# Expert blocks of over 64 rows: three fp32r passes over split operands, and a shorter ring of weights

## The chip, the cores and the metric

One Trainium2 chip, one core. The time is device microseconds of one execution of the whole program. An unchanged kernel's executions shown here lie between 2280.43 and 2285.77 us.

## What is computed

Two networks of two layers each run one after the other on 256 tokens of width 1024. The first network's layers have attention and then a mixture of experts; the second's have a mixer and a plain feed-forward. The change touches the experts alone. What they compute, from the reference:

```
def hier_moe(h, w_group, b_group, w_router, b_router, w1, w3, w2):
    ...                      # pick one of 4 groups, then 2 of its 8 experts, for each row of h
    def expert_block(a):
        xb, e = a            # up to 128 rows that chose expert e
        return (jax.nn.silu(xb @ w1[e]) * (xb @ w3[e])) @ w2[e]
    ...
    return jnp.zeros((t, d), h.dtype).at[tok_s].add(w_s[:, None].astype(h.dtype) * yb[dest])
```

There are 32 experts; w1 and w3 are 1024x512, w2 is 512x1024, all fp32. Layer 0 routes 512 rows (tokens and context), layer 1 routes 256, two experts to a row. How many rows an expert gets is known only during the run.

## The kernel before

**Stages.** build (L1623) runs layer 0's attention, its expert stage (moe_scope, L1580), layer 1's attention, its expert stage, and the second network. Inside moe_scope, route_tokens (L764) counts the rows of each expert and orders the experts: the even places from 2 on hold the large ones in falling size, the odd places small ones. Then experts (L984) goes through them with branches on the counts, all written out in a row: turn (L1117) takes an expert through tc.If; `small` (up to 64 rows: half1/half2 or, up to 32, quarter1/quarter2) or `large` (full1/full2 for 128 rows, and `rest` for each further 128).

**A full block.** full1 multiplies 128 gathered rows (xT, transposed, 8 slices of 128) with w1 (m = 0) and w3 (m = 1): 16 products of 128x128 by 128x512 into two PSUM banks (L1073). ScalarE takes Silu of the first bank (L1076), VectorE multiplies by the second (L1077). `between` runs next_rows, which transposes the next expert's rows (L997) and copies them to SBUF on ScalarE (L999). Four transposes (L1081) and a copy (L1082) make hT, and full2 multiplies it with w2 in 8 products (L1088); ScalarE and VectorE copy the result out (L1091, L1092) and GpSimd scatters it (L1002). All operands are plain fp32.

**Weights.** An expert's weights are six pieces of 128x2048 fp32, 1 MB each, loaded by SyncE's queue (wpiece, L139). The buffers are a ring (wtile, L132): WRING = 6 of a pool that lives for the whole program and nx more of one that lives for the expert stage, so 16 in layer 0 and 18 in layer 1. A piece is loaded when the buffer's last reader is through; for a large expert, whose readers stand in branches, that is the end of those branches.

**Order.** Instructions of one engine run in the order in which the program holds them. The tile framework fixes that order at build time by a simulated timeline: of what is ready it issues what was written first. Instructions inside a branch don't mix with those outside.

**The same arithmetic elsewhere.** The dense stages already use three passes: dense (L154) copies a weight to fp32r on ScalarE (L166), VectorE subtracts that from the weight to get the low part (L167), and mm3 (L176) adds high x high, high x low and low x high (L178 to L180):

```
    def mm3(self, out, xh, xl, wh, wl, start, stop):
        mm = self.nc.tensor.matmul
        mm(out, lhsT=xh, rhs=wh, start=start, stop=False)
        mm(out, lhsT=xh, rhs=wl, start=False, stop=False)
        mm(out, lhsT=xl, rhs=wh, start=False, stop=stop)
```

Of the kernel before, what the change touches and what calls it, by code (L numbers as in the profile page):

```python
# [9 lines left out]
F32 = mybir.dt.float32  # L10
F32R = mybir.dt.float32r
I32 = mybir.dt.int32
AF = mybir.ActivationFunctionType
ALU = mybir.AluOpType
# [5 lines left out]
P = 128  # L20
D = 1024
KT = 8
# [4 lines left out]
NE = 32  # L27
# [70 lines left out]
class Builder:  # L98
# [885 lines left out]
    def experts(self, l, nt, mp, first, meta, meta2, gtab, stabs, XG, XE, ybuf):  # L984
        tc, nc = self.tc, self.nc
# [21 lines left out]
        def w2slice(W, k, a, n):  # L1007
            return W[4 + k // 2][:, k % 2 * D + a:k % 2 * D + a + n]

        def wslice(W, m, k, a=0, n=512):  # L1010
            return W[2 * m + k // 4][:, k % 4 * 512 + a:k % 4 * 512 + a + n]
# [47 lines left out]
        def half2(c, W, hT):  # L1059
# [6 lines left out]
            nc.scalar.activation(ys, yb, AF.Copy)  # L1066
            scatter(1, c, ys)

        def full1(W, xT, hT, between):
            acc = [self.bankA() for _ in range(2)]  # L1070
            for m in range(2):
                for k in range(KT):
                    nc.tensor.matmul(acc[m], lhsT=xT[:, k], rhs=wslice(W, m, k), start=k == 0, stop=k == KT - 1)  # L1073
                if m == 0:
                    s = mp.tile([P, 512], F32, tag="s", name="s", bufs=1)
                    nc.scalar.activation(s, acc[0], AF.Silu)  # L1076
            nc.vector.tensor_tensor(s, s, acc[1], ALU.mult)  # L1077
            between()
            hb = self.bankB().rearrange("p (k t) -> p k t", k=4)
            for i in range(4):  # L1080
                nc.tensor.transpose(hb[:, i], s[:, i * P:i * P + P], self.ident)  # L1081
            nc.vector.tensor_copy(hT, hb)  # L1082

        def full2(c, W, hT):
            yb = [self.bankA() for _ in range(2)]
            for k in range(4):
                for m in range(2):
                    nc.tensor.matmul(yb[m], lhsT=hT[:, k], rhs=w2slice(W, k, m * 512, 512),  # L1088
                                     start=k == 0, stop=k == 3)
            ys = mp.tile([P, D], F32, tag="y0", name="ys", bufs=2)  # L1090
            nc.scalar.activation(ys[:, 0:512], yb[0], AF.Copy)  # L1091
            nc.vector.tensor_copy(ys[:, 512:1024], yb[1])  # L1092
            scatter(0, c, ys)

        def load(src, i, hi, **k):
            return nc.values_load(src[0:1, i:i + 1], min_val=0, max_val=hi,
                                  skip_runtime_bounds_check_because=MADE, **k)

        XT = [mp.tile([P, KT, P], F32, name=f"xt{i}_{l}") for i in range(2)]
        HT = [mp.tile([P, 4, P], F32, name=f"ht{i}_{l}") for i in range(2)]  # L1100
        first[1] += self.expert_weights(wm, load(meta2, 1, NE - 1, engines=[ENG.SP]), range(5, 6))
        rows_T(XG[0], XT[0])


        most = [(2 * T - 2) // (n + 1) for n in (64, 128, 256, 384)]

        sized = lambda k: "any" if k < 2 else "small" if k % 2 or (k - 2) // 2 >= most[0] else "large"
# [5 lines left out]
        def next_rows(k):  # L1113
            if k + 1 < NE:
                rows_T(XG[(k + 1) % AHEAD], XT[(k + 1) % 2], 64 if sized(k + 1) == "small" else P)

        def turn(k, kind, n, W):  # L1117

            i = (k - 2) // 2
            x = XT[k % 2]  # L1120
            groups = nt if kind == "any" else 1 + sum(i < m for m in most[1:nt]) if kind == "large" else 1
            m = meta2 if k > 1 else meta

            def block(g, size, b=lambda: None):

                ht = HT[(k + g) % 2]
                one, two = ((full1, full2), (half1, half2), (quarter1, quarter2))[size]
                one(W, x, ht, b)
                two(k * nt + g, W, ht)

            def rest(g):

                more = g + 1 < groups
                rows_T(XE, x)
                if more:
                    with tc.If(load(m, NE + k, T, engines=[ENG.Pool]) > P * (g + 1)):
                        gather(k * nt + g + 1, XE)
                if g > 1:
                    block(g, 0)
                else:  # L1140
                    with tc.If(n < P * g + 33) as fewer:
                        block(g, 2)
                    with fewer.Else():
                        with tc.If(n < P * g + 65) as few:
                            block(g, 1)
                        with few.Else():
                            block(g, 0)
                if more:
                    with tc.If(n > P * (g + 1)):
                        rest(g + 1)  # L1150

            def first(size):
                block(0, size, lambda: next_rows(k))

            def large():
                label = f"rest{l}_{k}"
                if groups > 1:
                    tc.mark_branch_hint_location(label, "LikelyTaken", [ENG.PE])
                    with tc.If(load(m, NE + k, T, engines=[ENG.Pool]) > P):
                        gather(k * nt + 1, XE)  # L1160
                first(0)
                if groups > 1:
                    with tc.If(n > P, label=label):
                        rest(1)

            def small():
                with tc.If(n > 32) as more:
                    first(1)
                with more.Else():
                    if k % 2 and k + 1 < NE and sized(k + 1) in ("large", "any"):  # L1170
                        tc.mark_branch_hint_location(f"either{l}_{k + 1}", "LikelyTaken", [ENG.PE])
                    first(2)

            if kind == "small":
                small()
            else:
                with tc.If(n < 65, label=f"either{l}_{k}") as fewer:
                    small()
                with fewer.Else():
                    large()  # L1180

        def pair(k):

            ahead(k)
            turn(k, sized(k), load(meta2, NE + k, T), self.expert_weights(wm, load(meta2, k, NE - 1, engines=[ENG.SP])))
            ahead(k + 1)
            n = load(meta2, NE + k + 1, T)
            with tc.If(n > 0) as some:
                W = self.expert_weights(wm, load(meta2, k + 1, NE - 1, engines=[ENG.SP]))
                turn(k + 1, "small", n, W)  # L1190
            with some.Else():
                next_rows(k + 1)
            if k + 2 < NE:
                with tc.If(load(meta2, NE + k + 2, T) > 0):
                    pair(k + 2)
# [384 lines left out]
    def moe_scope(self, l, nt):  # L1580
# [3 lines left out]
        with ExitStack() as ctx:  # L1584
# [5 lines left out]
            W = [self.expert_weights(wm, picked[0])]  # L1590
            self.banks(ctx, A=4, B=4)
            gp = self.after.enter_context(tc.tile_pool(name=f"mrows{l}", bufs=1, side="right"))
            mp = pool(name=f"moe{l}", bufs=1)
            nx = 10 if l == 0 else 12
            cw = ExitStack()
            self.wextra = (cw.enter_context(tc.tile_pool(name=f"wx{l}", bufs=nx)), nx)
            self.wcount = WRING
# [161 lines left out]
```

## Time and profile before

| | |
|---|---|
| median of 3 runs | 2283.38 us (2280.43 to 2285.77) |
| the profiled execution | 2275.24 us, its span 2272.8 |
| granted TensorE clock over the span | 0.923 |
| busy: TensorE / weight loads / VectorE / ScalarE / GpSimd | 84% / 59% / 44% / 32% / 12% |
| DMA | 456 MB, mean 201 GB/s |
| expert weights | 174 pieces of 1 MB: 15 experts in layer 0, 14 in layer 1 |

An engine's share is busy time over the span. Times of rows are us from the span's start. The expert stage's blocks run from 424.6 to 762 us in layer 0 and from 1033 to 1281 us in layer 1. A plain fp32 product shows as two records on TensorE, an fp32r pass as one. "Idle before" is time of that engine ahead of the instruction, with what ended it.

### The profile page before, as it was taken

How to read it: one execution, taken by the hardware profiler on the slowest of the kernel's cores; microseconds unless marked ns; L12 is line 12 of the kernel's file. 1: busy time of each engine (PE TensorE's matmuls, PEld its weight loads, DVE VectorE, ACT ScalarE, POOL GpSimd, SP SyncE). 2: the span in 40 equal slices, each digit the busy share in tenths (PEclk: the TensorE clock that was granted, in tenths of full speed). 3: DMA queues.
4: the chain of work that ended last, by engine and by line, in shares of the span. 5: the costliest groups of instructions: out<-in, count | busy, mean ns of one | idle time of the engine just before them, and what ended most of it. 6: DMA issues, size and time to landing. Idle time of an engine off the chain costs nothing. (4 is left out here: it accounts for less than half of the span.)

```text
span 2272.8 us, 27150 instructions
## 1 busy us (share of the span) xinstructions
PE 1916.9 (84%) x10066; PEld 1338.3 (59%) x10066; DVE 1006.2 (44%) x1968; ACT 732.1 (32%) x1304; POOL 263.4 (12%) x205
## 2 busy tenths in 40 slices
PE   6999797778886489967766479998999799998997
PEld 2656475433443177753333267786788677776886
DVE  3346655310000275661000257656554566566554
ACT  2233432100111254411101255444444454444442
POOL 0002401001101152120111102001000020002000
PEclk9999798799998799977988889999999999998999
DMA  9973214454779651156689754254455344444550
GB/s 395 378 294 127 105 38 180 174 197 186 310 283 402 254 219 44 40 222 266 263 326 411 286 191 146 96 196 170 167 186 184 129 163 145 134 164 166 185 178 26
DMA packets 74302, 456.06 MB, mean 201 GB/s; under 512 B 12696, under 2 KB 13244, under 8 KB 23648
## 3 DMA queue, kind: packets, MB, share of 16 engines
q1 hardware_dynamic: 61632, 430.99, 50.5%
q0 software_dynamic: 8816, 14.79, 1.8%
q10 hardware_dynamic: 3632, 7.37, 0.9%
q8 instruction: 133, 2.18, 0.4%
q14 instruction: 89, 0.73, 0.1%
HBM read 452.77 MB, written 13.30 MB: 205 GB/s over the span
## 5 line engine op out<-in xcount | busy, mean ns | idle before, releaser
L167 DVE TENSOR_TENSOR whl<-w,whl 128x1024 fp32r<-128x1024 f32 x312 | 396.4, 1284 | 230.1 <-ACT whl L166 220.3
L166 ACT ACTIVATE whl<-w 128x1024 fp32r<-128x1024 f32 x332 | 344.5, 1057 | 262.5 <-PE bankA L180 206.7
L178 PE MATMUL bankA<-whl,x2h 128*128 128x512 f32 (+1 forms) x864 | 344.3, 399 | 9.6 <-ACT x2h L238 7.2
L180 PE MATMUL bankA<-whl,x2l 128*128 128x512 f32 (+1 forms) x864 | 343.6, 398 | 5.8 <-DVE x2l L239 5.8
L179 PE MATMUL bankA<-whl,x2h 128*128 128x512 f32 (+1 forms) x864 | 341.1, 396 | 0.0
L178 PEld LDWEIGHTS bankA<-whl,x2h 128*128 128x128 f32 x864 | 167.8, 194 | 43.5 <-ACT x2h L238 8.2
L180 PEld LDWEIGHTS bankA<-whl,x2l 128*128 128x128 f32 x864 | 166.8, 193 | 40.4 <-DVE x2l L239 7.2
L1073 PE MATMUL bankA<-w,xt 128*128 128x512 f32 x320 | 155.3, 647 | 39.3 <-issue 31.5
L179 PEld LDWEIGHTS bankA<-whl,x2h 128*128 128x128 f32 x864 | 167.2, 194 | 34.3 <-issue 2.0
L1073 PEld LDWEIGHTS bankA<-w,xt 128*128 128x128 f32 x320 | 65.7, 208 | 126.4 <-issue 125.4
L178 PE MATMUL bankA<-whl,xh 128*128 128x512 f32 (+1 forms) x336 | 131.7, 392 | 5.1 <-ACT xh L238 5.1
L1020 PE MATMUL bankA<-w,xt 128*32 128x256 f32 x1216 | 88.4, 445 | 54.7 <-issue 47.2
L179 PE MATMUL bankA<-whl,xh 128*128 128x512 f32 (+1 forms) x336 | 128.7, 383 | 5.1 <-DVE whl L167 5.1
L180 PE MATMUL bankA<-whl,xl 128*128 128x512 f32 (+1 forms) x336 | 127.6, 384 | 0.0
L414 ACT ACTIVATE p<-bankS,sm 128x256 f32<-128x256 f32 (+2 forms) x160 | 85.6, 536 | 116.9 <-DVE sm L405 60.1
L213 POOL TENSOR_TENSOR sm<-sm,mhalf 128x1 f32<-128x1 f32 (+3 forms) x32 | 32.1, 1003 | 686.7 <-DVE sm L211 675.0
L1020 PEld LDWEIGHTS bankA<-w,xt 128*32 128x32 f32 x1216 | 48.9, 127 | 94.4 <-issue 74.6
L1077 DVE TENSOR_TENSOR s<-s,bankA 128x512 f32<-128x512 f32 x10 | 6.9, 688 | 200.6 <-PE bankA L1073 188.0
L1002 POOL DMA_INDIRECT ybuf<-ys,stab x34 | 34.8, 1023 | 499.7 <-ACT xt L999 124.8
L1024 DVE TENSOR_TENSOR s<-s,bankA 64x256 f32<-64x256 f32 x19 | 8.0, 423 | 177.0 <-ACT s L1023 177.0
L178 PEld LDWEIGHTS bankA<-whl,xh 128*128 128x128 f32 x336 | 63.8, 190 | 31.8 <-ACT xh L238 7.1
L1088 PE MATMUL bankA<-w,ht 128*128 128x512 f32 x160 | 71.3, 599 | 7.8 <-DVE ht L1082 7.8
(462 smaller groups left out, 2907.3 us busy)
## 6 DMA issues: line engine op xcount, KB each, us to landing
w<-in_wmoe SPq DMA_DIRECT2D x174, 1024.0 KB, 14.9
w<-in_wd SPq DMA_DIRECT2D x166, 1024.0 KB, 5.5
w<-in_wmod SPq DMA_DIRECT2D x48, 1024.0 KB, 9.1
y<-ybuf SPq DMA_DIRECT2D x12, 512.0 KB, 10.6
w<-in_rows SPq DMA_DIRECT2D x5, 1024.0 KB, 5.3
w<-mrow SPq DMA_DIRECT2D x7, 512.0 KB, 8.5
fbuf<-w SPq DMA_DIRECT2D x4, 512.0 KB, 2.9
nb<-in_nabias POOLq DMA_DIRECT2D x16, 128.0 KB, 2.4
```

What stands on the lines that cost most here:

```text
L166: nc.scalar.activation(h, s, AF.Copy)
L167: self.low = (eng or nc.vector).tensor_tensor(lo, s, h, ALU.subtract).ins
L178: mm(out, lhsT=xh, rhs=wh, start=start, stop=False)
L179: mm(out, lhsT=xh, rhs=wl, start=False, stop=False)
L180: mm(out, lhsT=xl, rhs=wh, start=False, stop=stop)
L213: self.power = self.nc.gpsimd.tensor_tensor(r, t, self.mhalf[:, :n], ALU.pow).ins
L414: nc.scalar.activation(p[:, :n], s[i][:, :n], AF.Exp, bias=nm[:, i:i + 1], accum_out=ss[:, i:i + 1])
L1002: nc.gpsimd.indirect_dma_start(out=ybuf.rearrange("r (m d) -> (r m) d", m=1 << parts), out_offset=bass.IndirectOffsetOnAxis(ap=stabs[parts ...
L1020: nc.tensor.matmul(acc[r:r + 32], lhsT=xT[:, k, 0:32], rhs=wslice(W, m, k, 256 * f, 256), start=k == 0, stop=k == KT - 1)
L1024: nc.vector.tensor_tensor(s, s, acc[64:128], ALU.mult)
L1073: nc.tensor.matmul(acc[m], lhsT=xT[:, k], rhs=wslice(W, m, k), start=k == 0, stop=k == KT - 1)
L1088: nc.tensor.matmul(yb[m], lhsT=hT[:, k], rhs=w2slice(W, k, m * 512, 512), start=k == 0, stop=k == 3)
```

## The change

Full blocks get their weights and rows as high and low parts. `split` copies 128x1024 of a weight piece to fp32r (ScalarE) and subtracts (VectorE) into one of three buffers; full1 does so for each two slices k, except the first two of m = 0, which stay plain fp32. split_rows does the same for the rows, into one pair of tiles XH and XL; next_split calls it for the next expert when that can be large. In full2 the first slice stays plain fp32, the other three are split. The output buffer of a full block is single instead of double. The ring has 7 extra buffers in place of 10 in layer 0 (13 in all) and 8 in place of 12 in layer 1 (14 in all).

```diff
--- before.py
+++ after.py
@@ -1066,28 +1066,55 @@
             nc.scalar.activation(ys, yb, AF.Copy)
             scatter(1, c, ys)
 
+        def split(w):
+
+            hl = mp.tile([P, 2, 1024], F32R, tag="whl", name="whl", bufs=3)
+            nc.scalar.activation(hl[:, 0], w, AF.Copy)
+            nc.vector.tensor_tensor(hl[:, 1], w, hl[:, 0], ALU.subtract)
+            return hl[:, 0], hl[:, 1]
+
+        def split_rows(x):
+
+            nc.scalar.activation(XH, x, AF.Copy)
+            nc.vector.tensor_tensor(XL, x, XH, ALU.subtract)
+
         def full1(W, xT, hT, between):
+
             acc = [self.bankA() for _ in range(2)]
             for m in range(2):
                 for k in range(KT):
-                    nc.tensor.matmul(acc[m], lhsT=xT[:, k], rhs=wslice(W, m, k), start=k == 0, stop=k == KT - 1)
+                    if m == 0 and k < 2:
+                        nc.tensor.matmul(acc[m], lhsT=xT[:, k], rhs=wslice(W, m, k), start=k == 0, stop=False)
+                        continue
+                    if k % 2 == 0:
+                        wh, wl = split(wslice(W, m, k, 0, 1024))
+                    c = slice(k % 2 * 512, k % 2 * 512 + 512)
+                    self.mm3(acc[m], XH[:, k], XL[:, k], wh[:, c], wl[:, c], k == 0, k == KT - 1)
                 if m == 0:
                     s = mp.tile([P, 512], F32, tag="s", name="s", bufs=1)
                     nc.scalar.activation(s, acc[0], AF.Silu)
+            self.w2 = split(w2slice(W, 1, 0, D))
             nc.vector.tensor_tensor(s, s, acc[1], ALU.mult)
             between()
             hb = self.bankB().rearrange("p (k t) -> p k t", k=4)
             for i in range(4):
                 nc.tensor.transpose(hb[:, i], s[:, i * P:i * P + P], self.ident)
-            nc.vector.tensor_copy(hT, hb)
+            nc.vector.tensor_copy(hT[:, 0], hb[:, 0])
+            nc.scalar.activation(HH, hb[:, 1:4], AF.Copy)
+            nc.vector.tensor_tensor(HL, hb[:, 1:4], HH, ALU.subtract)
 
         def full2(c, W, hT):
             yb = [self.bankA() for _ in range(2)]
             for k in range(4):
+                if k > 1:
+                    self.w2 = split(w2slice(W, k, 0, D))
                 for m in range(2):
-                    nc.tensor.matmul(yb[m], lhsT=hT[:, k], rhs=w2slice(W, k, m * 512, 512),
-                                     start=k == 0, stop=k == 3)
-            ys = mp.tile([P, D], F32, tag="y0", name="ys", bufs=2)
+                    if k == 0:
+                        nc.tensor.matmul(yb[m], lhsT=hT[:, 0], rhs=w2slice(W, 0, m * 512, 512), start=True, stop=False)
+                        continue
+                    wh, wl = (w[:, m * 512:m * 512 + 512] for w in self.w2)
+                    self.mm3(yb[m], HH[:, k - 1], HL[:, k - 1], wh, wl, False, k == 3)
+            ys = mp.tile([P, D], F32, tag="y0", name="ys", bufs=1)
             nc.scalar.activation(ys[:, 0:512], yb[0], AF.Copy)
             nc.vector.tensor_copy(ys[:, 512:1024], yb[1])
             scatter(0, c, ys)
@@ -1098,8 +1125,11 @@
 
         XT = [mp.tile([P, KT, P], F32, name=f"xt{i}_{l}") for i in range(2)]
         HT = [mp.tile([P, 4, P], F32, name=f"ht{i}_{l}") for i in range(2)]
+        XH, XL = (mp.tile([P, KT, P], F32R, name=f"{n}_{l}") for n in ("xth", "xtl"))
+        HH, HL = (mp.tile([P, 3, P], F32R, name=f"{n}_{l}") for n in ("hth", "htl"))
         first[1] += self.expert_weights(wm, load(meta2, 1, NE - 1, engines=[ENG.SP]), range(5, 6))
         rows_T(XG[0], XT[0])
+        split_rows(XT[0])
 
 
         most = [(2 * T - 2) // (n + 1) for n in (64, 128, 256, 384)]
@@ -1113,6 +1143,10 @@
         def next_rows(k):
             if k + 1 < NE:
                 rows_T(XG[(k + 1) % AHEAD], XT[(k + 1) % 2], 64 if sized(k + 1) == "small" else P)
+
+        def next_split(k):
+            if k + 1 < NE and sized(k + 1) != "small":
+                split_rows(XT[(k + 1) % 2])
 
         def turn(k, kind, n, W):
 
@@ -1126,6 +1160,8 @@
                 ht = HT[(k + g) % 2]
                 one, two = ((full1, full2), (half1, half2), (quarter1, quarter2))[size]
                 one(W, x, ht, b)
+                if g == 0:
+                    next_split(k)
                 two(k * nt + g, W, ht)
 
             def rest(g):
@@ -1136,6 +1172,7 @@
                     with tc.If(load(m, NE + k, T, engines=[ENG.Pool]) > P * (g + 1)):
                         gather(k * nt + g + 1, XE)
                 if g > 1:
+                    split_rows(x)
                     block(g, 0)
                 else:
                     with tc.If(n < P * g + 33) as fewer:
@@ -1144,6 +1181,7 @@
                         with tc.If(n < P * g + 65) as few:
                             block(g, 1)
                         with few.Else():
+                            split_rows(x)
                             block(g, 0)
                 if more:
                     with tc.If(n > P * (g + 1)):
@@ -1162,6 +1200,7 @@
                 if groups > 1:
                     with tc.If(n > P, label=label):
                         rest(1)
+                        next_split(k)
 
             def small():
                 with tc.If(n > 32) as more:
@@ -1190,6 +1229,7 @@
                 turn(k + 1, "small", n, W)
             with some.Else():
                 next_rows(k + 1)
+                next_split(k + 1)
             if k + 2 < NE:
                 with tc.If(load(meta2, NE + k + 2, T) > 0):
                     pair(k + 2)
@@ -1591,7 +1631,7 @@
             self.banks(ctx, A=4, B=4)
             gp = self.after.enter_context(tc.tile_pool(name=f"mrows{l}", bufs=1, side="right"))
             mp = pool(name=f"moe{l}", bufs=1)
-            nx = 10 if l == 0 else 12
+            nx = 7 if l == 0 else 8
             cw = ExitStack()
             self.wextra = (cw.enter_context(tc.tile_pool(name=f"wx{l}", bufs=nx)), nx)
             self.wcount = WRING
```

## Rows read from the trace of the kernel before

**Rows 1.** The page, part 1: busy us (share of the span) xinstructions.
```profile
PE 1916.9 (84%) x10066; PEld 1338.3 (59%) x10066; DVE 1006.2 (44%) x1968; ACT 732.1 (32%) x1304; POOL 263.4 (12%) x205
```

**Rows 2.** Windows of the expert stages: length, busy (count) by engine, clock, DMA, GB/s.
```profile
424.60:646.60 222.00, 184.37 (x844) 85.98 (x844) 24.64 (x36) 23.47 (x46) 19.65 (x19) 0.94 0.51 205
...
686.00:756.00 70.00, 50.93 (x453) 23.17 (x452) 3.97 (x10) 8.56 (x21) 10.07 (x10) 0.85 0.98 393
1033.00:1160.00 127.00, 102.41 (x453) 46.16 (x452) 8.22 (x15) 13.75 (x26) 11.07 (x11) 0.91 0.65 261
...
1165.00:1276.00 111.00, 71.31 (x824) 39.42 (x823) 6.31 (x17) 14.26 (x35) 16.02 (x17) 0.85 0.99 399
```

**Rows 3.** Waits of SyncE's DMA queue, 400 to 770: total us, times, longest.
```profile
SPq L143 <- PEq L1149: 143.4, 4, 47.2
...
SPq L143 <- PEq L1163: 40.4, 2, 28.2
```

**Rows 4.** Timeline of TensorE, layer 0: start, us, line, records [idle before].
```profile
526.21 14.00 PE L1073 MATMUL bankA<-w,xt 128*128 128x512 f32 x32 [0.25 <-ACT xt L999]
...
542.51 7.13 PE L1088 MATMUL bankA<-w,ht 128*128 128x512 f32 x16 [0.78 <-DVE ht L1082]
...
563.99 16.31 PE L1073 MATMUL bankA<-w,xt 128*128 128x512 f32 x32 [5.13 <-issue]
```

**Rows 5.** Timeline of TensorE in a dense stage, fp32r passes.
```profile
838.06 0.39 PE L180 MATMUL bankA<-whl,xl 128*128 128x512 f32 x1
...
838.74 0.39 PE L180 MATMUL bankA<-whl,xl 128*128 128x512 f32 x1
```

**Rows 6.** The page, part 5: groups, xcount | busy, mean ns | idle before.
```profile
L1073 PE MATMUL bankA<-w,xt 128*128 128x512 f32 x320 | 155.3, 647 | 39.3 <-issue 31.5
```

**Rows 7.** The page, part 5: the splits of the dense stages.
```profile
L167 DVE TENSOR_TENSOR whl<-w,whl 128x1024 fp32r<-128x1024 f32 x312 | 396.4, 1284 | 230.1 <-ACT whl L166 220.3
L166 ACT ACTIVATE whl<-w 128x1024 fp32r<-128x1024 f32 x332 | 344.5, 1057 | 262.5 <-PE bankA L180 206.7
```

**Rows 8.** Line L1177: ns min/median/max of its branches, first and last.
```profile
L1177 PEldq COMPARE_BRANCH  x17: 68/383/6785, 422.7 to 1255.7; - x17
L1177 DVEq COMPARE_BRANCH  x17: 43/56/72, 424.2 to 1254.7; - x17
L1177 ACTq COMPARE_BRANCH  x17: 34/45/59, 424.6 to 1257.0; - x17
```

**Rows 9.** Groups by form, 430 to 760: xcount | busy, mean ns | idle.
```profile
L1082 DVE COPY ht<-bankB 128x512 f32<-128x512 f32 x7 | 4.8, 691 | 5.3 <-PE bankB L1081 5.3
...
L1076 ACT ACTIVATE s<-bankA 128x512 f32<-128x512 f32 x7 | 4.2, 597 | 78.0 <-PE bankA L1073 78.0
...
L1030 DVE COPY ht<-bankB 128x128 f32<-128x128 f32 x9 | 2.6, 291 | 3.9 <-PE bankB L1029 3.9
```

**Rows 10.** Timeline of VectorE at the first expert of layer 0.
```profile
425.86 2.35 DVE L349 TENSOR_TENSOR hctx<-hctx,ln 128x1024 f32<-128x1024 f32 x2
```

**Rows 11.** Timeline of TensorE at the last large expert of layer 0.
```profile
655.71 4.10 PE L1073 MATMUL bankA<-w,xt 128*128 128x512 f32 x9 [0.45 <-ACT ys L1040]
```

**Rows 12.** Timeline of ScalarE at the same place.
```profile
655.33 0.38 ACT L1040 ACTIVATE ys<-bankA 128x256 f32<-128x256 f32 x1 [1.90 <-PE bankA L1037]
```

**Rows 13.** Timeline of TensorE among the small experts of layer 0.
```profile
716.32 6.58 PE L1020 MATMUL bankA<-w,xt 128*32 128x256 f32 x60 [2.38 <-DMA w<-in_wmoe]
```

**Rows 14.** Timeline of TensorE, the last products of layer 1's experts.
```profile
1277.12 3.65 PE L1063 MATMUL bankA<-w,ht 128*64 128x512 f32 x16 [0.52 <-DVE ht L1057]
```

**Rows 15.** Timeline of ScalarE in a feed-forward stage of the second network.
```profile
2150.41 1.06 ACT L166 ACTIVATE whl<-w 128x1024 fp32r<-128x1024 f32 x1 [0.30 <-PE bankA L180]
2151.77 0.38 ACT L238 ACTIVATE gh<-bankB 128x256 fp32r<-128x256 f32 x1 [0.29 <-PE bankB L225]
2152.05 0.38 ACT L1551 ACTIVATE gt<-bankA 128x256 f32<-128x256 f32 x1
2152.31 1.06 ACT L166 ACTIVATE whl<-w 128x1024 fp32r<-128x1024 f32 x1
```

## The prediction

> **What bounds the kernel now.** First the engine shares: TensorE is busy 84% of the span, no other engine half of it [rows 1]. That is a mean over stages, so next the stretches of the two expert stages. While large experts (over 64 rows) still come, 424.6 to 646.6 us in layer 0, TensorE is busy 184 of 222 us and the DMA share is only 0.51; layer 1 up to 1160 is alike (102 of 127 us, 0.65). When only small experts follow, the picture turns over: from 686 to 756 us and from 1165 to 1276 us the DMA share is 0.98 and 0.99 at 393 and 399 GB/s, while TensorE has gaps [rows 2]. The reader should see two regimes in one stage: first TensorE sets the pace, then the weight transfers do. The waits of the DMA queue say what joins them: SyncE stood 143 us, in four waits, behind the end of a large expert's branches (L1149) and 40 us behind L1163 [rows 3]. The ring is full, the next weights wait for a release, and a release comes when a large expert ends. So a faster large expert moves the start of the saturated stretch forward, and a shorter ring puts more bytes into it. The time follows from these two terms, and they have opposite signs.
>
> **The passes.** A product is one 128x128 by 128x512 step. In plain fp32 it leaves two records: a warm run of 16 products took 14.00 us (526.21), and the second half's 8 took 7.13 us [rows 4]. Taking the last record's overhang (0.59) off, (14.00 - 0.59)/31 x 2 = 0.865 and (7.13 - 0.59)/15 x 2 = 0.872; I take 0.86. In the dense stages three fp32r passes start 0.68 us apart from the first to the fourth (838.06 to 838.74) [rows 5]. The gain is 0.175 to 0.18 per product. A block turns 14 of 16 products of its first half and 6 of 8 of the second: 20 x 0.175 = 3.5 us. 320 records are 10 such blocks [rows 6]: 7 in layer 0, 3 in layer 1. The slower start of a run behind an idle stretch (16.31 us at 563.99, behind 5.13 of idle, against 14.00 [rows 4]) stays in either version.
>
> By the Trainium skill, "FP8 and Floating Point Precision", section TensorE Precision Notes, true fp32 is four passes through the array; three would then cost three quarters, 0.645 instead of 0.86, and save 0.215 each, 43 us over 200 products instead of 35. The rows contradict the price, not the count: a pass alone has a pitch of 0.227, where a quarter of the fp32 product is 0.215.
>
> **The splits.** A split is a ScalarE copy of 1.06 us and a VectorE subtraction, 1.28 in the mean, serving two products [rows 7]. TensorE eats that pair in 2 x 0.68 = 1.37, so VectorE just keeps up, with 0.1 to spare. Seven splits in the first half and three in the second are 12.8 us of VectorE; the split of the next rows is another. What hides them: the first two products are plain fp32, 1.7 us warm and 3.4 cold. ScalarE and VectorE usually arrive early, since TensorE alone pays at the branch: its longest L1177 took 6.8 us, ScalarE's and VectorE's under 0.08 [rows 8]. Three buffers can be filled in that time. From then on a split waits for TensorE to free a buffer, 1.06 + 1.28 = 2.3 us ahead of need, against two pairs in hand (2.7 us). I put 0.3 us of waiting at the turn to the second weight matrix, where Silu (0.60) [rows 9] also stands on ScalarE.
>
> Between the halves the copy of the transposed activations shrinks from 512 columns to 128 (0.69 to 0.29 [rows 9]); that would be 0.4 us, and I count 0.3, as it now queues behind a split. In the second half VectorE does the low part (384 columns, by those two rows 0.3 to 0.7), the low part of the next rows (1.28) and the third weight split (1.28), about 3.1 in a row and behind a ScalarE copy of some 0.5, where TensorE has 1.7 + 1.4 = 3.1 us of products that don't need the last of them: 0.6 us of stall. The ScalarE copies beside them are shorter. An ordinary block thus gains 3.5 + 0.3 - 0.3 - 0.6 = 2.9; I take 2.8. Its bounds are 3.9 (no stall) and about 0 (each split late by its own length once: the 2.9 of the slow rival below).
>
> Three blocks are not ordinary. The first of layer 0 finds VectorE in the residual's scaling until 428.2 [rows 10], with the low rows and first low weights behind it, ready near 430.8, while the two cold fp32 products that began at 424.6 end at 428.1: 2.5 lost, 0.3 gained. The one at 655.71 starts 0.45 us after the last copy of the block ahead [rows 11]; that copy ran on ScalarE until 655.71 [rows 12], so the split starts after it and its low part is ready 3.3 us later (a branch, 1.06 and 1.28), with 1.9 of cover: 1.4 gained. The block at 526.21 belongs to a second group of rows; their split now stands between its transposes and its products, with no waiting time ahead (0.25 us): 0. Together 7 x 2.8 + 0.3 + 1.4 + 0 = 21.3 us, 12.9 of them in layer 0.
>
> Splitting rows ahead of a large expert during a small one (2.3 us on two engines) lies beside TensorE's branch wait: 0, from 0 to +1 per expert if that wait goes. The single output buffer is 0: blocks lie over 20 us apart.
>
> **The ring.** Layer 0 goes from 16 buffers to 13, layer 1 from 18 to 14. Before the saturated stretch this costs nothing: when a large expert ends, one small expert's weights are already in, and the six that follow take 15 us, about the small one's time plus the branch. In the saturated stretch 3 and 4 more pieces of 1.05 MB must still come: at 393 and 399 GB/s [rows 2] 2.67 and 2.63 us each, 8.0 + 10.5 = 18.5 us. Does TensorE have slack to swallow that? In layer 0 it waits for a weight at 716.32, with 2.38 us of idle [rows 13], and is chained from there; in layer 1 the last half starts at 1277.12 [rows 14], 1 us after the stretch at 399 GB/s ends. So the cost is paid nearly in full. Bounds: 12 if layer 1 swallows most of its part, 20 if scatters and gathers slow the added pieces too.
>
> **The sum.** 18.5 - 21.3 = -2.8 us. On the profiled execution's 2275.24 us (span 2272.8) that is 2272.4; the median of the runs is 8.1 higher, so on 2283.38 it is 2280.6. A measurement of this kernel tells 0.2%, 4.6 us, from no change. The forecast is a near cancellation.
>
> **Rivals.**
> *All splits in time, faster.* Ten blocks at 3.3 give 33 - 18.5 = 14.5 less: 2269. For it: ScalarE and VectorE are busy for only 23 and 25 of 222 us [rows 2]. Against it: VectorE's margin per pair is 0.1 us, and three blocks have no head start.
> *Silu ahead of the splits, slower.* If ScalarE's order holds Silu of the first matrix ahead of the second's splits, TensorE waits at the turn for 0.60 + 1.06 + 1.28 = 2.9 us in each block: 29 lost, +26, 2309; half of that, where one split slips through, +12, 2295. It decides above 0.3 us per block, where the sum turns to a loss. Against it: in a later stage with the same helper ScalarE already mixes a split between the evacuations of the piece before (2150.41 to 2152.31 [rows 15]).
> *Branches of ScalarE and VectorE stall, slower.* Their code in a large branch grows several times, and TensorE's too (46 passes for 32 records in the first half). TensorE's stall of 6.8 us [rows 8] shows the price; four such on the splits' engines, with 3 us each uncovered, are +12, less the forecast's 2.8: +9, 2293. Against it: none so far exceeds 0.08. The Trainium skill, "Runtime: NRT & Kernel Launch", section Instruction fetch mechanics, has such a stall at a taken branch whose target page isn't loaded; TensorE's rows agree, the other two engines' don't show it yet.
> *Three quarters of the price.* With products 0.04 us cheaper than the rows have it, 8 us more are gained: 2273. The passes' rows are against it.
>
> **Chances.** Near cancellation 0.45 (own range 2274 to 2288), all splits in time 0.26, Silu first 0.14, branch stalls 0.12, three quarters 0.03. Split at 4.6 us: faster 0.15 + 0.24 + 0.03 = 0.42; same 0.25 + 0.02 + 0.02 = 0.29; slower 0.05 + 0.14 + 0.10 = 0.29. The range reaches from a gain of 17 (33 with the ring at 16) to a loss of 14 (the half case of Silu, and the ring at its upper bound): 2266 to 2297.
>
> **What would show it.** Right: a full first half near 13.5 us from cold and 11.5 warm, a second half near 6.2, the saturated stretches starting 11 and 8 us earlier in the expert stage and lasting 8 and 10 us longer. Wrong: TensorE idle by about 3 us at the turn between the weight matrices; an L1177 or L1167 of some us on ScalarE or VectorE; saturated stretches no longer than before, which would leave the full 21 us.

## The result, and the profile after

The changed kernel is slower: 2304.5 us median of four runs (2296.8 to 2313.8) against 2281.9, a ratio of 1.0096 [1.0075, 1.0117], some 22 us. The forecast was 2280.6, its range ended at 2297. The profiled execution took 2305.41 us, span 2303.6, mean granted clock 0.911 (before 0.923).

Part 1 of the page after, answering [rows 1]:
```profile
PE 1905.6 (83%) x10266; PEld 1383.9 (60%) x10266; DVE 1148.8 (50%) x2099; ACT 859.4 (37%) x1435; POOL 265.4 (12%) x205
```
TensorE is busy 11 us less in a span 31 us longer: it waits. The windows of the expert stages after, columns as in [rows 2]:
```profile
437.60:661.00 223.40, 176.59 (x1070) 113.96 (x1070) 96.60 (x104) 96.71 (x123) 23.47 (x21) 0.93 0.52 205
686.00:756.00 70.00, 40.29 (x453) 22.96 (x455) 5.31 (x11) 8.54 (x18) 9.98 (x10) 0.83 1.00 393
...
1048.40:1173.00 124.60, 99.86 (x512) 61.15 (x512) 48.21 (x51) 49.51 (x63) 11.26 (x11) 0.86 0.59 231
1182.00:1300.00 118.00, 66.47 (x769) 34.04 (x763) 9.43 (x18) 14.55 (x32) 16.01 (x16) 0.83 1.00 404
```
The two regimes stand, the DMA share still goes from about half to 1.00. But the stretches of large experts, which the passes should have shortened by some 20 us, are hardly shorter. In a table, from TensorE's first and last product of each layer's experts (us; a "block" is a full one; the last three columns are experiments told below):

| stretch | before | after | ring_short | ordered | bias_later |
|---|---|---|---|---|---|
| start to the end of the last routing table (L964) | 423.7 | 427.6 | 428.8 | 425.6 | 428.3 |
| to layer 0's first product | 0.9 | 10.0 | 0.9 | 10.0 | 0.9 |
| to the end of its last block | 256.1 | 247.7 | 253.1 | 238.8 | 234.3 |
| to its last product | 81.3 | 92.6 | 90.3 | 91.8 | 95.1 |
| to layer 1's first product | 271.0 | 270.5 | 279.9 | 273.2 | 273.6 |
| to the end of its last block | 126.8 | 125.1 | 121.7 | 111.7 | 115.7 |
| to its last product | 121.0 | 136.1 | 133.7 | 136.3 | 135.8 |
| to the end | 992.0 | 994.0 | 990.1 | 990.8 | 993.9 |

Three things stand out: 9.1 us of waiting ahead of the first expert, which no step forecast; stretches of blocks shorter by 8.4 and 1.7 us where ten blocks were to give 21 in all; and stretches behind them longer by 11.3 and 15.1. The first row, where the programs are alike, shows how far single profiles differ: 423.7 to 428.8; a second profile of the kernel before (below) has 426.1.

Inside a block, VectorE of the changed kernel between the halves of the second expert (start, us, line):
```profile
492.34 1.23 DVE L1073 TENSOR_TENSOR whl<-w,whl 128x1024 fp32r<-128x1024 f32 x1 [0.35 <-ACT whl L1072]
493.48 0.68 DVE L1097 TENSOR_TENSOR s<-s,bankA 128x512 f32<-128x512 f32 x1
494.07 1.22 DVE L1079 TENSOR_TENSOR xtl<-xt,xth 128x1024 fp32r<-128x1024 f32 x1
495.21 1.22 DVE L1073 TENSOR_TENSOR whl<-w,whl 128x1024 fp32r<-128x1024 f32 x1
496.35 0.29 DVE L1102 COPY ht<-bankB 128x128 f32<-128x128 f32 x1
497.19 0.56 DVE L1104 TENSOR_TENSOR htl<-bankB,hth 128x384 fp32r<-128x384 f32 x1 [0.56 <-ACT hth L1103]
```
Before, the two short instructions that TensorE waits for at this place (the product with the gate, and the copy of the hidden rows) were VectorE's only work there:
```profile
488.75 0.69 DVE L1077 TENSOR_TENSOR s<-s,bankA 128x512 f32<-128x512 f32 x1 [22.59 <-PE bankA L1073]
490.19 0.69 DVE L1082 COPY ht<-bankB 128x512 f32<-128x512 f32 x1 [0.75 <-PE bankB L1081]
```
Now the low part of the last but one piece of the second matrix (L1073 at 492.34) stands ahead of the product with the gate (L1097), which starts 0.9 us after TensorE's last pass (492.56) instead of 0.1. The low parts of the next rows (L1079) and of the last piece (L1073 at 495.21), which TensorE needs only at the end of the second half, stand ahead of the copy (L1102), on which the second half's first product waits. TensorE waits twice, for L1097 and, with the transposes done, for L1102:
```profile
494.22 0.66 PE L1101 MATMUL bankB<-cst,s 128*128 128x128 f32 x4 [1.66 <-DVE s L1097]
496.69 3.61 PE L1113 MATMUL bankA<-w,ht 128*128 128x512 f32 x4 [1.81 <-DVE ht L1102]
```
The gap between the halves grew from 2.3 us to 2.96 to 2.99 in seven blocks and 4.10 to 4.13 in three (those with the next rows' low part in it). In the seven most of it is the late product with the gate; the last piece's low part runs beside the transposes there and holds the copy up by only 0.3 us. And the second halves fall into two kinds: four of 6.1 us, six of 7.5 to 7.8. The six run partly at the lower of the two clock levels, 1.2 GHz. TensorE in this block (length, busy, granted clock):
```profile
496.00:500.00 4.00, 3.31 (x5) 0.57 0.06 25
```

### The profile page after: what moved, and what is told of

Its sections match the earlier page's. It is cut to its first block, busy times and chain, and to the rows that moved or that the text cites. A ratio compares the mean times of both kernels' runs of the same rounds, so it can differ in the third digit from the quotient of the medians.

```text
span 2303.6 us, 27976 instructions
## 1 busy us (share of the span) xinstructions
PE 1905.6 (83%) x10266; PEld 1383.9 (60%) x10266; DVE 1148.8 (50%) x2099; ACT 859.4 (37%) x1435; POOL 265.4 (12%) x205
## 5 line engine op out<-in xcount | busy, mean ns | idle before, releaser
L167 DVE TENSOR_TENSOR whl<-w,whl 128x1024 fp32r<-128x1024 f32 x312 | 398.1, 1290 | 232.6 <-ACT whl L166 222.0
L166 ACT ACTIVATE whl<-w 128x1024 fp32r<-128x1024 f32 x332 | 344.5, 1057 | 261.9 <-PE bankA L180 207.6
L1073 DVE TENSOR_TENSOR whl<-w,whl 128x1024 fp32r<-128x1024 f32 x100 | 118.9, 1222 | 66.8 <-ACT whl L1072 66.3
L1072 ACT ACTIVATE whl<-w 128x1024 fp32r<-128x1024 f32 x100 | 102.4, 1054 | 32.5 <-PE bankA L180 24.5
L178 PEld LDWEIGHTS bankA<-whl,xh 128*128 128x128 f32 x336 | 64.2, 191 | 32.8 <-ACT xh L238 7.3
L179 PEld LDWEIGHTS bankA<-whl,xh 128*128 128x128 f32 x336 | 64.2, 191 | 17.4 <-DVE whl L167 6.1
L180 PEld LDWEIGHTS bankA<-whl,xl 128*128 128x128 f32 x336 | 63.7, 189 | 16.5 <-issue 4.8
```

Of the source, the lines that this page charges most:

```text
L166: nc.scalar.activation(h, s, AF.Copy)
L167: self.low = (eng or nc.vector).tensor_tensor(lo, s, h, ALU.subtract).ins
L1072: nc.scalar.activation(hl[:, 0], w, AF.Copy)
L1073: nc.vector.tensor_tensor(hl[:, 1], w, hl[:, 0], ALU.subtract)
```

## The experiments

All were timed against the kernel before on the same chip, whose medians there were 2281.3 to 2284.7; us are (ratio - 1) x 2283.

| run | median | ratio | us |
|---|---|---|---|
| changed kernel | 2304.5 | 1.0096 [1.0075, 1.0117] | +21.9 |
| ring_short | 2299.7 | 1.0072 [1.0056, 1.0089] | +16.4 |
| ring_l0 | 2295.8 | 1.0062 [1.0040, 1.0084] | +14.2 |
| ring_l1 | 2286.9 | 1.0017 [1.0002, 1.0031] | +3.9 |
| order_rows | 2300.4 | 1.0090 [1.0062, 1.0117] | +20.5 |
| order_w2 | 2283.8 | 1.0004 [0.9988, 1.0020] | +0.9 |
| ordered | 2277.8 | 0.9982 [0.9963, 1.0000] | -4.1 |
| first_only | 2290.6 | 1.0040 [1.0025, 1.0055] | +9.1 |
| gap_only | 2304.4 | 1.0110 [1.0093, 1.0127] | +25.1 |
| gains_pool | 2303.4 | 1.0082 [1.0055, 1.0110] | +18.7 |
| start_only | 2298.6 | 1.0074 [1.0057, 1.0091] | +16.9 |
| bias_later | 2270.8 | 0.9944 [0.9925, 0.9963] | -12.8 |
| bias_later_ring | 2270.4 | 0.9947 [0.9928, 0.9966] | -12.1 |
| halves | 2287.9 | 1.0024 [1.0007, 1.0041] | +5.5 |

**The ring alone.** The kernel before with shorter rings (`ring_l0`: 7 and 12; `ring_l1`: 10 and 8):
```diff
-            nx = 10 if l == 0 else 12
+            nx = 7 if l == 0 else 8
```


> The kernel before with one edit: the extra ring of 10 (layer 0) and 12 (layer 1) pieces cut to 7 and 8; products stay fp32, no splits. The prediction's step: three and four pieces less cost 8.0 + 10.5 = 18.5 us, all behind the last full block of each layer, so about 2300 us. The accounting from the two traces (the stretch behind the last full block grew by 10.0 us in layer 0 and 15.1 in layer 1): +25, about 2307. Rival, the growth of those stretches comes from the splits and the later start and not from the ring: below +6, about 2286.

> The kernel before with only layer 1's extra ring cut, from 12 to 8. The prediction's step: four pieces in layer 1 cost 10.5 us, 2292; with ring_short's 18.4 the three of layer 0 are then 8. Rival: by the profiles of before and ring_short layer 1's experts grew by 7.6 us and layer 0's by 6.0, the rest of the 18.4 lying outside of the experts: 2288 to 2289 here.

> The kernel before with only layer 0's extra ring cut, from 10 to 7 pieces. The prediction's step gave 8.0 us: 2290. If the costs of the two layers add up to ring_short's 18.4 and layer 1's is 3.4: 15, 2297. Rival: what each layer loses is partly lost once, 2290 with 3.4 from the other layer and the rest only when both are short.

> The kernel before once more, for a second profile. If its stages are steady, the first expert starts at about 424.6 us, the experts take 337 and 248 us; if single profiles spread by some us per stage, growth of 2 to 5 us between two profiles says nothing.

Together +16.4, where the prediction's term was 18.5; layer 0 alone +14.2 [9.1, 19.2], layer 1 alone +3.9 [0.5, 7.1]. The costs add up, but they are not shared out as forecast (8.0 and 10.5). In the profiles the stretches behind the last block grew as forecast, 81.3 to 90.3 and 121.0 to 133.7 (the second profile of before has 81.3 and 121.1), but layer 1's stretch of blocks got 5 us shorter, and 9 us appear between the layers. With one ring cut, its own layer's stretch grows alone: to 89.0 in `ring_l0`, to 133.9 in `ring_l1`. One side effect is visible: with the shorter ring SyncE takes up a gate row's transfer (L1213) early and stands there for VectorE's L350.
```profile
SPq L1213 <- DVE hctx L350: 52.2, 1, 52.2
```
Layer 0's blocks did not get longer by it (253.1 against 256.1). Where the rest of layer 0's 14 us lies is not settled.

**The passes alone.** The changed kernel without the splits of weights:
```diff
         def split(w):
...
+            nc.scalar.activation(seen, w[:, 0:1], AF.Copy)
+            return fixed[:, 0], fixed[:, 1]
```


> The changed kernel with its short ring, its three passes, its split rows and split hidden rows, but without the splits of weights: every pass reads one fixed pair of high and low tiles made once per layer, and a one-column copy on ScalarE stands where a half piece was split, so that pieces are still released by a reader. What is left out: the products are not those of the experts' weights. If the passes are worth the 3.5 us per full block of the prediction and nothing but the splits takes it away, ten blocks give 35 less 25 for the ring: about 2272. If the passes give nothing on TensorE (the granted clock falls, the branches stay), the ring remains: about 2305. The full blocks in the profile tell: 21 to 22 us each (passes work) or 24 to 25.

Layer 1 can't be read here: its experts are picked from altered values, and it ran five full blocks instead of three; so the time (2236.0) counts for nothing. Layer 0 can: an undisturbed first half takes 11.5 us, a second 6.1, where the prediction had 11.5 and 6.2. TensorE in such a half:
```profile
610.61 0.40 PE L178 MATMUL bankA<-wfix,xth 128*128 128x512 f32 x1
610.85 0.39 PE L179 MATMUL bankA<-wfix,xth 128*128 128x512 f32 x1
611.08 0.40 PE L180 MATMUL bankA<-wfix,xtl 128*128 128x512 f32 x1
611.31 0.39 PE L178 MATMUL bankA<-wfix,xth 128*128 128x512 f32 x1
```
Three passes take 0.70, near the 0.68 of [rows 5]. By the Trainium skill, "FP8 and Floating Point Precision", TensorE Precision Notes, fp32 is four passes; three take 0.81 of its 0.865 here, not three quarters.

**The order on VectorE.** `ordered` queues the low parts of the next rows and of the second matrix's last two pieces behind the low part of the hidden rows; `order_rows` only the next rows', `order_w2` only the second matrix's (cuts of the edit):
```diff
+            with low_after():
+                nc.vector.tensor_tensor(hl[:, 1], w, hl[:, 0], ALU.subtract)
...
+            return tc.issue_after(behind[0]) if behind else nullcontext()
...
+            with low_after():
+                nc.vector.tensor_tensor(XL, x, XH, ALU.subtract)
...
+            self.lowhid = nc.vector.tensor_tensor(HL, hb[:, 1:4], HH, ALU.subtract).ins
...
+                    behind[:] = [self.lowhid]
                     self.w2 = split(w2slice(W, k, 0, D))
...
+                    behind[:] = [] if size else [self.lowhid]
                     next_split(k)
```


> The changed kernel with one edit: on VectorE the low parts of the next rows and of the last two pieces of the second matrix are queued behind the low part of the hidden rows, instead of ahead of the copy of the hidden rows. Theory: these two subtractions of 1.22 us ahead of that copy make the gap between the two halves of a full block (2.3 us before, 2.9 to 4.1 after) and, through it, the half clock of the second half; the gap goes back to about 2.4 and six second halves from 7.6 to 6.2: -10 (gaps) -8 (clock), about 2288. Rival: the gap only moves into the second half, which then waits for its own low parts: within 4 us of the changed kernel's 2304.

> The changed kernel with half of the edit of ordered: only the low part of the next rows (L1079) is queued behind the hidden rows' low part; the last two pieces of the second matrix stay ahead of the copy of the hidden rows. If the next rows alone make the loss, about 2278 as ordered. If both count by their 1.22 us, the gap falls only in the three blocks with next rows at that place, from 4.1 to 2.9, and the half clock stays in most second halves: about 2298.

> The changed kernel with the other half of the edit of ordered: only the low parts of the last two pieces of the second matrix are queued behind the hidden rows' low part; the next rows' low part stays ahead of the copy of the hidden rows. If the two halves add up: 2304.5 - 22.6, about 2282. If the order pays only when both are out of the way (the clock needs the short gap in every block): 2290 to 2298.

The same work in another order is 26.0 us faster (21.9 to -4.1); the second matrix's pieces make 21 of it; the rows alone make 1.4 by the ratios (4 by the medians). By the intervals, neither these nor what is left over can be told from nothing. VectorE and TensorE of `ordered` at the same place, then the window:
```profile
492.68 0.69 DVE L1104 TENSOR_TENSOR s<-s,bankA 128x512 f32<-128x512 f32 x1 [0.63 <-PE bankA L180]
494.12 0.29 DVE L1109 COPY ht<-bankB 128x128 f32<-128x128 f32 x1 [0.75 <-PE bankB L1108]
494.97 0.56 DVE L1111 TENSOR_TENSOR htl<-bankB,hth 128x384 fp32r<-128x384 f32 x1 [0.56 <-ACT hth L1110]
495.44 1.22 DVE L1086 TENSOR_TENSOR xtl<-xt,xth 128x1024 fp32r<-128x1024 f32 x1
496.57 2.35 DVE L1074 TENSOR_TENSOR whl<-w,whl 128x1024 fp32r<-128x1024 f32 x2
```
```profile
494.46 1.98 PE L1122 MATMUL bankA<-w,ht 128*128 128x512 f32 x4 [0.39 <-DVE ht L1109]
```
```profile
496.00:500.00 4.00, 4.00 (x19) 1.00 0.02 6
```
All ten gaps are 1.82 or 1.83 us, all ten second halves 6.1 us, at the full clock. In the changed kernel gaps sum to 33.2, second halves to 70.5; here to 18.2 and 61.1, while the first halves sum to 145.8 in both: 24.4 us of the 26.0 that were timed. In `order_w2` the gap is 1.82 us in seven blocks and 2.38 in three, and one second half of ten is slow; in `order_rows` no gap is under 2.96, and seven second halves are slow.

**Is the clock the gap's doing?** Three needless subtracts ahead of the copy, in the kernel before; and three passes in the first matrix alone:
```diff
+            for i in range(3):
+                with tc.issue_after(last):
+                    last = nc.vector.tensor_tensor(idle, w, w, ALU.subtract).ins
...
+            with tc.issue_after(last):
+                nc.vector.tensor_copy(hT, hb)
```


> The kernel before with one addition: three VectorE subtracts of 128 x 512 (some 0.65 us each), whose result nobody reads, between the product with the gate and the copy of the hidden rows in every full block; products fp32, ring long. They take 1.95 us of which the transposes hide about 0.75, so the gap between the halves goes from 2.3 to about 3.5: +12 over ten blocks, about 2293. Theory of the clock: in the changed kernel second halves behind gaps of 3 to 4 us run partly at the half clock; if it is the gap, second halves here take more than 7.13 us and the time comes to 2300 or more. Rival: the passes with their splits draw the clock down, and fp32 halves stay at 7.13 us.

> The changed kernel with three passes in the first matrix alone: the second matrix stays fp32, its splits and those of the hidden rows are gone, the ring stays short. Second halves of 7.13 us and gaps of about 2.3 (3.5 where the next rows' low part stands ahead of the copy). Against ordered (6.1 and 1.8): about +15, 2293. Against the changed kernel: -10, that is, the second matrix's passes cost more than they gave there. Rival: if the half clock of the second halves comes from the passes of the first matrix and not from the gap, the second halves here run cold too (above 9 us): 2305 or more.

In `gap_only` gaps are 3.5 to 3.6 us, and three of ten fp32 second halves take 8.83 us instead of 7.13, at a lowered clock:
```profile
496.63 8.83 PE L1094 MATMUL bankA<-w,ht 128*128 128x512 f32 x16 [2.02 <-DVE ht L1088]
```
```profile
496.00:500.00 4.00, 3.37 (x6) 0.74 0.02 4
```
So neither passes nor splits are needed for it. But seven halves behind the same gap stayed warm: the gap allows the fall and does not decide it. Gaps (+12.3) and clock (3 x 1.7) make 17 of the 25 us; the stretch behind layer 0's last block was also 91.4 us there, with the long ring, and why is open. `first_only` is 12.8 us faster than the changed kernel with fewer passes: what the second matrix's passes saved there, their place in VectorE's order cost, and more.

**The first wait.** VectorE, ScalarE and TensorE of the changed kernel at layer 0's first expert:
```profile
432.03 2.35 DVE L350 TENSOR_TENSOR hlat<-hlat,ln 128x1024 f32<-128x1024 f32 x2
434.31 2.35 DVE L350 TENSOR_TENSOR hctx<-hctx,ln 128x1024 f32<-128x1024 f32 x2
```
```profile
436.90 1.08 ACT L999 ACTIVATE xt<-bankB 128x512 f32<-128x512 f32 x2 [40.60 <-DVE hctx L350]
```
```profile
437.60 3.75 PE L1087 MATMUL bankA<-w,xt 128*128 128x512 f32 x4 [11.26 <-ACT xt L999]
```
The copy of the first rows has no data from L350. What joins them is, as far as the sizes tell, memory: by the sizes in the diff the new tiles of layer 0 take 7 KB of a partition more than the shorter ring gives up, and the larger pool then reaches the bias and gain rows that L349 and L350 read. The addresses themselves stand in no trace. Before, the bias passes ran at 461 us, in idle time; now they come before any expert tile is written. `gains_pool` packs the tiles 6 KB tighter, to end below the rows, and moves the passes to GpSimd; `start_only` packs them and puts the bias passes behind the first block on VectorE; `bias_later` is that together with `ordered`:
```diff
-        HT = [mp.tile([P, 4, P], F32, name=f"ht{i}_{l}") for i in range(2)]
+        HT = [mp.tile([P, 2 * P], F32, name=f"ht{i}_{l}") for i in range(2)]
...
-                        self.gain_bias(self.h(tt), *rows, self.nc.vector)
+                        self.nc.vector.tensor_tensor(self.h(tt), self.h(tt), rows[0], ALU.mult)
...
                 two(k * nt + g, W, ht)
+                if self.lnrows and k == 0 and g == 0:
+                    for tt in range(nt):
+                        nc.vector.tensor_tensor(self.h(tt), self.h(tt), self.lnrows[1], ALU.add)
```


> The changed kernel with its expert tiles packed 6 KB tighter, so that they no longer reach the memory of layer 0's gain and bias rows, and with the four gain and four bias passes of layer 0 (L349, L350) on GpSimd instead of VectorE. Theory: in the changed kernel the first expert waits 11 us for VectorE's L350, whose rows lie where its tiles go; with memory and engine freed its first product starts at about 425 to 429 us of the span instead of 437.6: -9, about 2295. Rival 1: the start comes earlier, but the wait is taken up by the first expert's weights or by the ring: less than 3 us. Rival 2: GpSimd's 19 us of passes hold back the gathers behind them, and the first expert's second block waits for its rows: no gain, up to +5.

> The changed kernel with the edits of bias_later on memory and on layer 0's bias passes, but with VectorE's order in the full blocks as it was in the changed kernel. Theory: the wait of the first expert is worth by itself what it gave on top of ordered (2277.8 to 2270.8) or the whole 9.1 us: 2295 to 2298. Rival: the wait was hidden behind the first weights: 2302 or more.

> The kernel ordered, with its expert tiles packed 6 KB tighter, so that they end below layer 0's gain and bias rows, and with the four bias passes of layer 0 on VectorE moved from ahead of the first expert to behind its first block. Theory: the first product follows the last table (L964) by 1.2 us, as in the kernel before, instead of 10.3, and the first low part by about 8 instead of 14; 5 to 9 us from the 2277.8 of ordered, about 2271. Rival: the stretch behind layer 0's last full block is bound by transfers and takes it all: 2277 to 2278.

In all three the first product follows L964 by 0.9 us again, so the wait was L350's. All three pack the tiles and move the bias passes at once; that memory, and not their place in the queue, made the order is not shown by itself. `start_only` is 5.0 us faster than the changed kernel, within the intervals, and `bias_later` 8.7 faster than `ordered`; the wait was 9.1 in the profiles. `gains_pool` gained 3, within its interval, and not as any of its three theories had it. Its VectorE, then its GpSimd, in the first block:
```profile
430.86 22.57 DVE L1073 TENSOR_TENSOR whl<-w,whl 128x1024 fp32r<-128x1024 f32 x6
```
```profile
433.12 6.68 POOL L349 TENSOR_TENSOR hctx<-hctx,ln 128x1024 f32<-128x1024 f32 x2
```
Six subtracts took 22.57 us, where six of 1.22 are 7.3: four took 3.4 each, one 1.21 while GpSimd issued a gather, and one 8.17 beside three more of its passes. GpSimd's passes beside the first four took 3.34 each instead of 2.34. That block's first half took 30.4 us and gave the 9 back. By the Trainium skill, "SBUF — State Buffer", section Who interferes with whom, a VectorE instruction with two SBUF inputs contends with a GpSimd instruction that reads SBUF, under a lock held for a whole instruction; the trace agrees, with both engines at some 3.4 us an instruction and one subtract held for 8.17.

**Buying ring back.** `bias_later_ring` gives layer 1 one more piece; `halves` (on `ordered`) splits in 512 columns, which frees 8 KB for one more piece in each layer:
```diff
-            hl = mp.tile([P, 2, 1024], F32R, tag="whl", name="whl", bufs=3)
+            hl = mp.tile([P, 2, 512], F32R, tag="whl", name="whl", bufs=4)
```


> The kernel bias_later with the memory that packing freed in layer 1 given to its ring: 9 extra pieces instead of 8. By the price per piece of ring_short (2.6 us) 2268; rival, as halves with one piece more in each layer hinted: no gain from one piece, 2270 to 2272.

> The kernel ordered, with each split made in two of 512 columns over four buffers of 4 KB instead of three of 8 KB; the 8 KB freed go to the ring: 8 and 9 extra pieces instead of 7 and 8. By the ring's price per piece (18.4 us for seven pieces, 2.6 each) 5 us less than ordered, about 2272.5. Rival: twice the instructions on ScalarE and VectorE (16 low parts per first half at some 0.65 us or more against 14 products of 0.68) make the splits the bound: full first halves of 14 us or more, 2280 or above.

No gain from one piece, as ring_l1 would have it. `halves` is 10 us slower than `ordered`, but not by its rival: its low parts take 687 ns each, and layer 0's first halves are shorter in sum (96.1 against 103.7 us). Its profile loses in layer 1 (251.5 against 248.0), behind layer 0's last block (96.0 against 91.8) and ahead of the experts, where the programs are alike. Not settled.

## Why the prediction was wrong

**The regimes and the ring: right in sum.** Large experts still set the releases; SyncE's waits after, answering [rows 3]:
```profile
SPq L143 <- DVEq L1187: 149.5, 4, 55.0
```
The ring's term was 18.5; alone it measured 16.4 [12.8, 20.3]. "Before the saturated stretch this costs nothing" is not shown, since the layers came out at 14.2 and 3.9.

**The passes: right.** 11.5 and 6.1 us without splits.

**"VectorE just keeps up": nearly.** In `ordered` an undisturbed first half takes 13.0 us, 1.5 more than with fixed parts: 0.7 us of waits and 0.71 of the next rows' transposes, which the planner moved from the gap, where they cost nothing, to behind the first two products (TensorE of `ordered`):
```profile
616.62 0.71 PE L997 MATMUL bankB<-cst,xg 64*128 64x64 f32 x8
```
A block there takes 13.0 + 1.8 + 6.1 = 20.9 us. Before, the block at this place took 25.1, but it started cold behind a wait for weights, and the one in `ordered` did not:
```profile
612.85 15.67 PE L1073 MATMUL bankA<-w,xt 128*128 128x512 f32 x32 [4.88 <-DMA w<-in_wmoe]
```
```profile
614.73 1.96 PE L1094 MATMUL bankA<-w,xt 128*128 128x512 f32 x4 [0.46 <-ACT ys L1040]
```
The one block of before that ran at the full clock and without waits (526.21, [rows 4]) took 14.0 + 2.3 + 7.1 = 23.4. Like with like the gain is 2.5 us; 2.8 was forecast.

**"Near 13.5 us from cold": not reached.** In the changed kernel the six first halves that ran partly at the lower clock level took 14.0 to 17.1 us, with fixed parts two in layer 0 took 14.4. The one at 573.16 took 16.7, no less than the same expert before (16.31 at 563.99), as the clock stayed at the lower level for 8.8 us of it instead of 4.7. TensorE there after, then before:
```profile
572.00:582.00 10.00, 8.84 (x22) 0.50 1.01 419
```
```profile
564.00:574.00 10.00, 10.00 (x18) 0.77 1.02 415
```
Why it stayed low is not shown. In sum the ten first halves went from 156.7 to 145.8 us, 10.9 less; the forecast has 13.8 for them (21.3 less 0.75 for the rest of each block).

**The step that failed: the gap.** The prediction let the hidden rows' copy queue "behind a split" for 0.1 us, and put the next rows' low part and the third split behind it, "about 3.1 in a row", in the second half: 0.6 us of stall. On the chip both stood ahead of the copy, and the second split ahead of the product with the gate. The diff's order of lines was read as the engine's order, though a planner writes that order, and nothing in the change tied it. The stall thus fell where nothing covers it, 0.7 to 1.8 us a block on the gap of before, and the longer gap let the clock fall in six second halves, 1.4 to 1.7 us each. In its own terms the gap and the second half were to give 0.75 us a block (0.3 + 1.05 - 0.6). They took 9.4 us before and 10.4 after, a loss of 0.9; in `ordered` they take 7.9, a gain of 1.5. Nowhere did the prediction price a clock that falls between the halves of a block, though [rows 4] show the price of a cold start (16.31 for 14.00).

**The second: the first expert.** "2.5 lost, 0.3 gained" took [rows 10] for the end of VectorE's residual work and counted its data (by its own times, 430.8 - 428.1, it is 2.7). L350, which ran later before, now came first, as far as can be told because the larger pool reaches its rows: 9.1 us in the profiles, 5 to 9 as timed.

**The chain.** By the ratios: ring +16.4; passes and splits with order and start mended (ring_short to bias_later) -29.2; the first wait +8.7; the order +26.0: +21.9. Forecast were +18.5 and -21.3. The -29.2 is more than the price of the passes: it also holds a gap half a us shorter than before and fewer cold starts. In the profiles the ten blocks (both halves and the gap between) sum to 251.1 us before, 249.5 after and 225.1 in `ordered`. So the passes were worth about what was forecast, and two waits that the change does not name ate the gain.

**The rivals.** Silu did not stand ahead of the splits; ScalarE of the changed kernel at the turn:
```profile
485.55 1.06 ACT L1072 ACTIVATE whl<-w 128x1024 fp32r<-128x1024 f32 x1 [0.39 <-PE bankA L180]
486.91 0.60 ACT L1095 ACTIVATE s<-bankA 128x512 f32<-128x512 f32 x1 [0.30 <-PE bankA L180]
487.41 2.00 ACT L1072 ACTIVATE whl<-w 128x1024 fp32r<-128x1024 f32 x2
```
Its price of 2.9 us a block was near the 2.6 that the order cost; its place was not: the queue that mattered was VectorE's, half a block later. The branches of the split engines stayed short, as in [rows 8]:
```profile
L1216 PEldq COMPARE_BRANCH  x17: 68/384/4907, 426.6 to 1271.8; - x17
L1216 ACTq COMPARE_BRANCH  x17: 34/45/59, 438.6 to 1272.8; - x17
L1216 DVEq COMPARE_BRANCH  x17: 43/56/72, 439.8 to 1271.5; - x17
```
"All splits in time" (2269) is what the change gives once both waits are gone: `bias_later`, 2270.8, is faster than either kernel.

## What to carry to other kernels

When a planner writes an engine's order, new work on that engine can land ahead of the short instructions that another engine waits for; name those instructions, and tie the new work behind them. A larger pool can also move deadlines: here work that read the memory it grew into came ahead of the pool's first write, though it has nothing to do with that data. Price a wait on TensorE with the clock that may follow it.

## What the runs showed of the hardware

After a gap of 3 to 4 us between two dense runs of products the granted clock can fall, with fp32 products and with passes: of 119 gaps of 1.8 to 2.4 us between the halves of a block, in twelve profiles, one was followed by a slow second half; of 53 between 2.8 and 4.1 us, in six (after, start_only, gains_pool, order_rows, first_only, gap_only), thirty-one. With passes 27 of 40 were, with fp32 second halves 4 of 13, so the length of the gap is not all that counts. VectorE and GpSimd subtracting or multiplying tensors in SBUF at the same time slowed each other from 1.22 and 2.34 us to about 3.4, and once one subtract to 8.17.
